# Both score products over all 128 rows: the keys' rounding remainder kept twice, and a smaller DMA scratch

## The chip, the cores and the metric

The kernel runs on one core of one Trainium2 chip. The metric is the device time of one execution in microseconds (us). Times of single instructions are in nanoseconds (ns) where the profile gives them so. TensorE is PE in the profile (PEld is its weight load), VectorE is DVE, ScalarE is ACT, GpSimd is POOL and SyncE is SP.

## The reference, cut to what matters

Three layers over 2048 tokens of width 1024: sliding-window attention, a gated recurrence, and a hybrid of two recurrences. The change touches the first layer alone. Its attention has 16 query heads of 64 in two groups of eight, two key/value heads, blocks of 128 queries, and a window that reaches into the block before:

```python
s = jnp.einsum('bqhgd,bkhd->bhgqk', qi, ki, preferred_element_type=jnp.float32) * scale
s = jnp.where(band & ((idx > 0) | (k_rel >= ATTN_BLOCK)), s, -jnp.inf)
m = jnp.maximum(jnp.max(s, axis=-1), sink)
p = jnp.exp(s - m[..., None])
p = p / (jnp.sum(p, axis=-1) + jnp.exp(sink - m))[..., None]
out = jnp.einsum('bhgqk,bkhd->bqhgd', p, vi)
```

## The kernel before

**Work and phases.** The 2048 tokens are cut into four quarters of 512. Each layer is worked a quarter at a time, in an order written out by hand (`00 01 10 02 d0 11 03 d1 ...`: layer, quarter), so attention stands in the first 480 us (quarters 0 and 1), around 825 to 1035 us (quarter 2) and around 1575 to 1800 us (quarter 3), beside other work.

**Products in two parts.** A float32 operand is kept as a rounded part (`F32R`, the name ends in `h` or the tile's first half) and as what the rounding left out (`l`). A projection is three products per 128 rows: hi·hi, hi·lo, lo·hi (`psA`, `psB`).

**Scores.** `attn_pair` works one query head of each group (`g` = 0, 1) at a time. Its tile `q[g]` (written in `q_evac`, named `qs` in the profile) has 128 rows: in the half `H2[g]` the rounded query of 64 rows, in the other half what its rounding left out. `kh[g]` holds the rounded key of key head `g` in both halves, so one product over 128 rows gives q_hi·k_hi + q_lo·k_hi. `kl` holds the key's remainder: key head 0 in rows 0 to 63, key head 1 in rows 64 to 127. A second product over the 64 rows `H2[g]` adds q_hi·k_lo to the same bank. A pair has 4 blocks (`block(b)`, 128 queries by up to 256 keys), a quarter has 8 pairs: 4·8·4·2 = 256 products with `kh` and 256 with `kl`.

**Behind the scores.** DVE adds the mask and takes the row maximum, ACT takes the exponential, DVE divides, PE transposes (`psPT`), ACT copies (`PT`), and PE multiplies with the values (`psO`).

**Keys.** `k_evac` runs once per quarter. From the second quarter on it first copies the last 128 columns of `kh` and `kl` to the front; then it rotates the key, and writes `kh` (four ACT copies of 64 rows x 512) and `kl` (two DVE subtractions).

**The order of the work.** The main thread (projections and output products) and side threads (`chains` for attention, `norms`, `ends`) are interleaved by a planner (`Pace`, `Threads`): each step has a due time from a table of costs, and a tile framework then places each engine's instructions. The planner's cost of an `F32R` product is its columns over 2400 MHz, whatever its rows.

All recorded operations have line L251 in the profile, so groups are read by tile names.

Of the kernel before, what the change touches and what calls it, by code (L numbers as in the profile page):

```python
# [10 lines left out]
F32 = mybir.dt.float32  # L11
F32R = mybir.dt.float32r
# [3 lines left out]
ALU = mybir.AluOpType  # L16
# [4 lines left out]
P = 128  # L21
D = 1024
TQ = 512
# [286 lines left out]
def rec_stack(ctx: ExitStack, tc: tile.TileContext, A, out, T=2048, layers=(0, 1, 2)):  # L310
    nc = tc.nc
    NPH = T // TQ
    pace = Pace(tc)
    te, ve, se, ge, sy = (pace.engine(e, n) for e, n in (
        (nc.tensor, "pe"), (nc.vector, "dve"), (nc.scalar, "act"), (nc.gpsimd, "pool"), (nc.sync, "dma")))
# [7 lines left out]
    st = ctx.enter_context(tc.tile_pool(name="st", bufs=1))  # L323
# [198 lines left out]
    H2 = [slice(0, 64), slice(64, 128)]  # L522
# [272 lines left out]
    if 0 in layers:  # L795
        aw, awo = A["attn_w_in"][0], A["attn_w_out"][0]
        ab = A["attn_b_in"][0]

        kh = [st.tile([P, P + TQ], F32R, name=f"kh{g}") for g in range(2)]
        kl = st.tile([P, P + TQ], F32R, name="kl")  # L800
        V0 = st.tile([P, 5, P], F32, name="V0")
    SWAP = [(i + 8 if i < 8 else i - 8) if i < 16 else i for i in range(32)]

# [53 lines left out]
    def layer0(i, ph, seq):  # L857

        S_ = {}

        def k_evac(ps):
            if ph:
                yield from need(("chain", seq - 1))
                for t in (*kh, kl):
                    se.copy(t[:, :P], t[:, TQ:].bitcast(F32))
                ve.tensor_copy(V0[:, 0], V0[:, 4])
            S_["tabs"] = yield from rope_tables(ph)
            k = yield from big.take([P, TQ], F32, "k0")
            yield from rope(k, ps, C["bkv"][:, 0:1], S_["tabs"])
            for g in range(2):  # L870
                for half in H2:
                    se.copy(kh[g][half, P:], k[H2[g]])
                ve.tensor_tensor(kl[H2[g], P:], k[H2[g]], kh[g][H2[g], P:].bitcast(F32), ALU.subtract)
            big.give(k)

        def v_evac(ps):
            vT = yield from big.take([P, TQ], F32, "vT")
            se.activation(out=vT, in_=ps, func=AF.Identity, bias=C["bkv"][:, 1:2])
            psd.give(ps)
            S_["vT"] = vT  # L880
            done.add(("v", i))

        def q_evac(pr):
            def go(ps):
                q = yield from big.take([P, TQ], F32, "q")
                yield from rope(q, ps, C["bq"][:, pr:pr + 1], S_["tabs"])

                S_["q", pr] = []
                for g in range(2):
                    t = yield from big.take([P, TQ], F32R, "qs")  # L890
                    se.copy(t[H2[g]], q[H2[g]])
                    ve.tensor_tensor(t[H2[1 - g]], q[H2[g]], t[H2[g]].bitcast(F32), ALU.subtract)
                    S_["q", pr].append(t)
                big.give(q)
                done.add(("q", i, pr))
                if pr == 7:
                    big.give(*S_["tabs"])
            return go

        def z_evac(pr):  # L900
            def go(ps):
                tz = yield from big.take([P, TQ], F32, "tz")
                se.activation(out=tz, in_=ps, func=AF.Tanh, bias=C["bzh"][:, pr:pr + 1], scale=0.5)
                ve.tensor_scalar(tz, tz, 0.5, 0.5, ALU.mult, ALU.add)
                ve.scalar_tensor_tensor(tz, ps, C["bz"][:, pr:pr + 1], tz, ALU.add, ALU.mult)
                psd.give(ps)
                S_["z", pr] = tz
                done.add(("z", i, pr))
            return go

        def w_out(half, cb):
            csl = slice(256 * cb, 256 * cb + 256)
            return 4, [(slice(64 * g, 64 * g + 64), slice(0, 256),
                        awo[512 * g + 256 * half:512 * g + 256 * half + 256, csl].rearrange("(k r) c -> r k c", r=64)) for g in range(2)], ("awo", half, cb)

        qs = [ch(i, w_ch(aw, 64 * pr, 512 + 64 * pr), q_evac(pr), ("chain", seq + pr - 2)) for pr in range(8)]
        zs = [ch(i, w_ch(aw, 1280 + 64 * pr, 1792 + 64 * pr), z_evac(pr), ("chain", seq + pr - 2)) for pr in range(8)]
        halves = [out_half(i, h, [w_out(h, cb) for cb in range(4)], A["attn_b_out"][0]) for h in range(2)]
        head = [ch_two(i, ch(i, w_ch(aw, 1024), k_evac), ch(i, w_ch(aw, 1152), v_evac)), qs[0], zs[0], qs[1]]
        body = []  # L920
        for pr in range(1, 6):
            body.append(zs[pr])
            if pr == 5:
                body += halves[0]
            body.append(qs[pr + 1])
        body += [zs[6], ch_two(i, qs[7], zs[7], True)]

        def chains():
            big.kept = 5
            yield from need(("v", i))  # L930
            yield pace.there(S_["vT"])
            ps = yield from bank(psm, "psV")
            for b in range(4):
                te.transpose(ps[:, P * b:P * b + P], S_["vT"][:, P * b:P * b + P], ident)
            yield
            se.copy(V0[:, 1:].rearrange("p a b -> p (a b)"), ps)
            psm.give(ps)
            big.give(S_["vT"])
            for pr in range(8):
                yield from attn_pair(ph, i, pr, S_)  # L940
                done.add(("chain", seq + pr))

        return head, body, halves[1], chains, 8

    def attn_pair(ph, i, pr, S_):
        yield from need(("q", i, pr))
        q = S_["q", pr]
# [3 lines left out]
        def block(b):  # L951

            k0 = 0 if (ph or b) else P
            S = yield from big.take([P, 2, 2 * P + 1], F32, "S", own=True)
            pss = []
            pss.append((yield from bank(psm, "psS", ahead=1)))
            pss.append((yield from bank(psm, "psS")))
            for g in range(2):
                te.matmul(pss[g][:, k0:2 * P], lhsT=q[g][:, P * b:P * b + P], rhs=kh[g][:, P * b + k0:P * b + 2 * P], start=True, stop=False)
            for g in range(2):  # L960
                te.matmul(pss[g][:, k0:2 * P], lhsT=q[g][H2[g], P * b:P * b + P], rhs=kl[H2[g], P * b + k0:P * b + 2 * P], start=False, stop=True)
            left[0] -= 1
            if not left[0]:
                big.give(*q)
            se.copy(S[:, :, 2 * P], C["sink"][:, pr])
            yield

            nm = sm.tile([P, 2], F32, tag="nm", name="nm")
            den = sm.tile([P, 2], F32, tag="den", name="den")
            for g in range(2):  # L970
                ve.tensor_tensor_reduce(out=S[:, g, k0:2 * P], in0=pss[g][:, k0:2 * P], in1=C["amask"][:, k0:], scale=-0.125,
                                        scalar=C["sink"][:, pr, g:g + 1], op0=ALU.add, op1=ALU.min, accum_out=nm[:, g:g + 1])
                psm.give(pss[g])
            yield
            for g in range(2):
                se.activation(out=S[:, g, k0:], in_=S[:, g, k0:], func=AF.Exp, bias=nm[:, g:g + 1], scale=-1.0, accum_out=den[:, g:g + 1])
            yield
            ve.reciprocal(den, den)
            for g in range(2):
                ve.tensor_scalar(S[:, g, k0:2 * P], S[:, g, k0:2 * P], den[:, g:g + 1], None, ALU.mult)  # L980
            yield
            bk = yield from bank(psm, "psPT")
            pt = bk.rearrange("p (k g q) -> p k g q", k=2, g=2)
            kbs = [1] if k0 else [0, 1]
            for kb in kbs:
                for g in range(2):
                    te.transpose(pt[:, kb, g], S[:, g, P * kb:P * kb + P], ident)
            big.give(S)
            yield
            PT = yield from big.take([P, 2, 2, P], F32, "PT", own=True)  # L990
            se.copy(PT[:, kbs[0]:], pt[:, kbs[0]:])
            psm.give(bk)
            yield
            if not po:
                po.append(None)
                po[0] = yield from bank(psm, "psO")
            if po[0] is None:
                yield lambda: po[0] is not None
            for kb in kbs:
                for g in range(2):  # L1000
                    te.matmul(po[0][64 * g:64 * g + 64, P * b:P * b + P], lhsT=V0[:, b + kb, 64 * g:64 * g + 64],
                              rhs=PT[:, kb, g], start=(kb == kbs[0]), stop=(kb == 1))
            big.give(PT)
# [859 lines left out]
```

## Time and profile before

| | |
|---|---|
| median of 3 runs | 3697.05 us (3694.93 to 3703.11) |
| the profiled execution's own time | 3696.45 us |
| its span, first to last instruction | 3694.7 us |
| mean granted clock of TensorE | 0.973 |
| PE, PEld, DVE, ACT, POOL busy | 95%, 80%, 65%, 35%, 12% |

The 1.75 us between the profiled execution's time and its span lie around the first and last instructions. A busy share is an average over stages that have different limits; and a matmul counts as busy from its start to its modelled end, so PE can be busy all the time and still have its matmuls far apart. The distance of matmul starts tells more than their durations.

### The profile page before, as it was taken

The numbers are of one execution on the slowest core, as the hardware profiler recorded it, in microseconds if no ns is written. First come the engines' busy times: TensorE is split into PE (matmuls) and PEld (weight loads), VectorE is DVE, ScalarE is ACT, GpSimd is POOL, SyncE is SP. The second block draws the span as 40 slices with busy tenths as digits, with TensorE's granted clock in tenths as the row PEclk, the third lists the DMA queues.
The fourth block names the chain that finished last, engine by engine and source line by source line (L and its number), as shares of the span: only waits on it lengthen the run. The fifth ranks groups of instructions, "written<-read, shape, count | busy, mean of one in ns | idle before, by whom it ended". The sixth has DMA issues, their size and how long they took to land. (4 is left out here: it accounts for less than half of the span.)

```text
span 3694.7 us, 75897 instructions
## 1 busy us (share of the span) xinstructions
PE 3521.4 (95%) x30488; PEld 2965.9 (80%) x30488; DVE 2402.3 (65%) x6735; ACT 1298.8 (35%) x3370; POOL 444.6 (12%) x649
## 2 busy tenths in 40 slices
PE   5999999989998999999999999999999999999998
PEld 4788887878887878877878787788778888878888
DVE  4666566466555677776666767665776765665675
ACT  4555433344432222343322223432232242334222
POOL 3421034421033000000000002110000010011000
PEclk8999999999998999999999999999999999999999
DMA  6766466755367444453575345485434457544665
GB/s 170 199 185 208 142 202 226 230 172 196 133 223 271 168 134 137 155 174 109 177 252 169 130 126 172 136 293 191 147 125 132 147 180 254 189 161 152 229 217 200
DMA packets 351104, 666.34 MB, mean 180 GB/s; under 512 B 164640, under 2 KB 246560, under 8 KB 298016
## 3 DMA queue, kind: packets, MB, share of 16 engines
q1 hardware_dynamic: 350752, 661.49, 54.1%
q8 instruction: 240, 3.93, 0.4%
q14 instruction: 112, 0.92, 0.1%
HBM read 494.42 MB, written 166.99 MB: 179 GB/s over the span
## 5 line engine op out<-in xcount | busy, mean ns | idle before, releaser
L251 PE MATMUL psA<-hth,wp 128*128 128x512 f32 (+1 forms) x5120 | 1560.6, 374 | 50.1 <-ACT wp L251 32.2
L251 PEld LDWEIGHTS psA<-hth,wp 128*128 128x128 f32 x5120 | 933.1, 193 | 218.7 <-ACT wp L251 33.7
L251 PE MATMUL psA<-htl,wp 128*128 128x512 f32 (+1 forms) x2560 | 935.3, 365 | 0.0
L251 PE MATMUL psB<-wp,mgh 128*128 128x256 f32 x3072 | 593.5, 292 | 14.3 <-DVE y L251 6.3
L251 PEld LDWEIGHTS psA<-htl,wp 128*128 128x128 f32 x2560 | 494.4, 193 | 62.2 <-issue 2.9
L251 PEld LDWEIGHTS psB<-wp,mgh 128*128 128x128 f32 x3072 | 487.6, 193 | 29.3 <-DVE y L251 7.8
L251 POOL TENSOR_TENSOR wp<-wf,wp 128x256 fp32r<-128x256 f32 x412 | 348.6, 877 | 934.8 <-ACT wp L251 827.1
L251 PE MATMUL psB<-wp,mgl 128*128 128x256 f32 x1536 | 443.5, 289 | 0.2 <-DVE mgl L251 0.2
L251 PE MATMUL psB<-wp,hth 128*128 128x256 f32 x1536 | 309.6, 297 | 4.3 <-DMA wp<-wk 3.9
L251 PEld LDWEIGHTS psB<-wp,mgl 128*128 128x128 f32 x1536 | 295.6, 193 | 3.3 <-issue 1.2
L251 PEld LDWEIGHTS psB<-wp,hth 128*128 128x128 f32 x1536 | 244.4, 194 | 13.5 <-issue 3.7
L251 PE MATMUL psB<-wp,htl 128*128 128x256 f32 x768 | 222.9, 290 | 0.0
L251 DVE TENSOR_TENSOR pr<-X,Mb 128x16 f32<-128x16 f32 (+30 forms) x496 | 205.2, 414 | 11.4 <-POOL Mb L251 1.7
L251 DVE TENSOR_TENSOR y<-psB,y 128x256 f32<-128x256 f32 x256 | 97.8, 419 | 111.8 <-PE psB L251 111.1
L251 DVE SCALAR_TENSOR_TENSOR Sbd<-Sbd,WC,psSt 64x64 f32<-64x64 f32 x256 | 71.4, 279 | 136.1 <-PE psSt L251 132.5
L251 ACT ACTIVATE S<-S,nm 128x257 f32<-128x257 f32 (+1 forms) x256 | 127.2, 499 | 82.9 <-DVE nm L251 82.0
L251 DVE TENSOR_REDUCE X<-pr 128x8 f32<-128x16 f32 (+30 forms) x496 | 146.6, 295 | 10.3
L251 ACT ACTIVATE junk<-y 128x1024 bf16<-128x1024 f32 (+1 forms) x128 | 94.5, 738 | 165.2 <-DVE y L251 154.4
L251 PEld LDWEIGHTS psB<-wp,htl 128*128 128x128 f32 x768 | 148.7, 194 | 2.5 <-issue 1.1
L251 DVE CUSTOM_DVE_ANT_0 S<-psS,amask,sink 128x256 f32<-128x256 f32 (+1 forms) x256 | 114.7, 471 | 41.2 <-PE psS L251 39.8
L251 DVE TENSOR_TENSOR QR<-QR,T 128x256 f32<-128x256 f32 x192 | 87.5, 456 | 80.0 <-PE psL L251 71.8
L251 POOL MEMSET Xt<- 32x256 f32 x32 | 9.7, 308 | 1055.8 <-PE psM L251 544.9
(283 smaller groups left out, 5442.6 us busy)
## 6 DMA issues: line engine op xcount, KB each, us to landing
wp<-wk SPq DMA_DIRECT2D x309, 1024.0 KB, 5.0
wk<-wp SPq DMA_DIRECT2D x103, 1024.0 KB, 5.0
xin<-x SPq DMA_DIRECT2D x48, 512.0 KB, 5.8
wf<-in_rec_w_in_dram SPq DMA_DIRECT2D x32, 512.0 KB, 6.3
x<-y SPq DMA_DIRECT2D x32, 512.0 KB, 6.1
wf<-in_w_in_dram SPq DMA_DIRECT2D x29, 512.0 KB, 6.7
ud<-um SPq DMA_DIRECT2D x52, 256.0 KB, 4.0
u<-ud SPq DMA_DIRECT2D x48, 256.0 KB, 3.2
```

The lines of the kernel that those rows point to most:

```text
L251: r = f(*a, **k)
```

## The change

`kl` becomes a list of two tiles, `kl[g]`. The remainder is still written by DVE into the half `H2[g]`, and an ACT copy puts it into the other half too. The second score product reads all 128 rows of `q[g]` and `kl[g]`, so it gives q_hi·k_lo + q_lo·k_lo. The two products of one `g` now follow each other in the code; before, both `kh` products came first. The carry at the start of a quarter copies four tiles instead of three. The program reserves 2048 bytes per partition for dynamic DMA instead of the default 16384; the second `kl` tile takes 2560.

```diff
--- before.py
+++ after.py
@@ -797,7 +797,7 @@
         ab = A["attn_b_in"][0]
 
         kh = [st.tile([P, P + TQ], F32R, name=f"kh{g}") for g in range(2)]
-        kl = st.tile([P, P + TQ], F32R, name="kl")
+        kl = [st.tile([P, P + TQ], F32R, name=f"kl{g}") for g in range(2)]
         V0 = st.tile([P, 5, P], F32, name="V0")
     SWAP = [(i + 8 if i < 8 else i - 8) if i < 16 else i for i in range(32)]
 
@@ -861,7 +861,7 @@
         def k_evac(ps):
             if ph:
                 yield from need(("chain", seq - 1))
-                for t in (*kh, kl):
+                for t in (*kh, *kl):
                     se.copy(t[:, :P], t[:, TQ:].bitcast(F32))
                 ve.tensor_copy(V0[:, 0], V0[:, 4])
             S_["tabs"] = yield from rope_tables(ph)
@@ -870,7 +870,8 @@
             for g in range(2):
                 for half in H2:
                     se.copy(kh[g][half, P:], k[H2[g]])
-                ve.tensor_tensor(kl[H2[g], P:], k[H2[g]], kh[g][H2[g], P:].bitcast(F32), ALU.subtract)
+                ve.tensor_tensor(kl[g][H2[g], P:], k[H2[g]], kh[g][H2[g], P:].bitcast(F32), ALU.subtract)
+                se.copy(kl[g][H2[1 - g], P:], kl[g][H2[g], P:].bitcast(F32))
             big.give(k)
 
         def v_evac(ps):
@@ -956,9 +957,8 @@
             pss.append((yield from bank(psm, "psS", ahead=1)))
             pss.append((yield from bank(psm, "psS")))
             for g in range(2):
-                te.matmul(pss[g][:, k0:2 * P], lhsT=q[g][:, P * b:P * b + P], rhs=kh[g][:, P * b + k0:P * b + 2 * P], start=True, stop=False)
-            for g in range(2):
-                te.matmul(pss[g][:, k0:2 * P], lhsT=q[g][H2[g], P * b:P * b + P], rhs=kl[H2[g], P * b + k0:P * b + 2 * P], start=False, stop=True)
+                for n, part in enumerate((kh, kl)):
+                    te.matmul(pss[g][:, k0:2 * P], lhsT=q[g][:, P * b:P * b + P], rhs=part[g][:, P * b + k0:P * b + 2 * P], start=(n == 0), stop=(n == 1))
             left[0] -= 1
             if not left[0]:
                 big.give(*q)
@@ -1843,7 +1843,7 @@
     import concourse.bacc as bacc
     from concourse.bass_utils import run_bass_kernel_spmd
 
-    nc = bacc.Bacc("TRN2", target_bir_lowering=False, num_devices=1)
+    nc = bacc.Bacc("TRN2", target_bir_lowering=False, num_devices=1, dynamic_dma_scratch_size=2048)
     arrays, args = {}, {}
 
     def add(key, name, a):
```

What stands in PE's order for two blocks of scores that follow an output projection (in the second quarter; `kh_89` and `kh_90` are the two key heads; the number behind a name is the tile's). Before:

```order
L251 MATMUL psB<-wp,mgl 128x256
L251 MATMUL psS<-kh_89,qs 128x256
L251 MATMUL psS<-kh_90,qs 128x256
L251 MATMUL psS<-kl,qs 128x256 x2
L251 MATMUL psS<-kh_89,qs 128x256
L251 MATMUL psS<-kh_90,qs 128x256
L251 MATMUL psS<-kl,qs 128x256 x2
L251 MATMUL psA<-hth,wp 128x512
L251 MATMUL psA<-htl,wp 128x512
```

and now (`kl_91` and `kl_92` are the two remainder tiles):

```order
L251 MATMUL psB<-wp,mgl 128x256
L251 MATMUL psS<-kh_89,qs 128x256
L251 MATMUL psS<-kl_91,qs 128x256
L251 MATMUL psS<-kh_90,qs 128x256
L251 MATMUL psS<-kl_92,qs 128x256
L251 MATMUL psS<-kh_89,qs 128x256
L251 MATMUL psS<-kl_91,qs 128x256
L251 MATMUL psS<-kh_90,qs 128x256
L251 MATMUL psS<-kl_92,qs 128x256
L251 MATMUL psA<-hth,wp 128x512
L251 MATMUL psA<-htl,wp 128x512
```

Before, the four products of a block stand as kh, kh, kl, kl; now as kh, kl, kh, kl. The count of products is the same.

At the end of the first quarter, PE's order where the scores stand between the products of a projection. Before:

```order
L251 MATMUL psA<-htl,wp 128x256
L251 MATMUL psS<-kh_90,qs 128x256
L251 MATMUL psPT<-ident,S 128x128
L251 MATMUL psS<-kl,qs 128x256
L251 MATMUL psPT<-ident,S 128x128
L251 MATMUL psA<-hth,wp 128x256
L251 MATMUL psS<-kh_89,qs 128x256
L251 MATMUL psS<-kl,qs 128x256
L251 MATMUL psA<-hth,wp 128x256
L251 MATMUL psS<-kh_90,qs 128x256
L251 MATMUL psS<-kl,qs 128x256
L251 MATMUL psA<-htl,wp 128x256
```

and now:

```order
L251 MATMUL psA<-hth,wp 128x256
L251 MATMUL psS<-kh_89,qs 128x256
L251 MATMUL psS<-kl_91,qs 128x256
L251 MATMUL psS<-kh_89,qs 128x256
L251 MATMUL psS<-kl_91,qs 128x256
L251 MATMUL psS<-kh_90,qs 128x256
L251 MATMUL psS<-kl_92,qs 128x256
L251 MATMUL psA<-hth,wp 128x256
L251 MATMUL psS<-kh_90,qs 128x256
L251 MATMUL psS<-kl_92,qs 128x256
L251 MATMUL psA<-htl,wp 128x256
```

Before, a pair kh, kl of one key head stands alone between products of the projection, and once a transpose lies between its two halves; now three pairs stand in a row and a fourth follows one product later.

What stands on ACT at the start of the third quarter (`k` is the rotated key, `qs` the query tile that the first score reads). Before:

```order
L251 CAST kh_89<-k_8773 64x512 x2
L251 ACTIVATE mt<-psO_8695,hrs 128x128 x4
L251 ACT_TABLE_LOAD
L251 ACTIVATE tz<-psA,bzh 128x512
L251 CAST kh_90<-k_8773 64x512 x2
L251 CAST mgh<-g_8381 128x512
L251 CAST qs<-q 64x512 x2
```

and now:

```order
L251 CAST kh_89<-k_8780 64x512 x2
L251 ACTIVATE mt<-psO_8701,hrs 128x128 x4
L251 ACT_TABLE_LOAD
L251 ACTIVATE tz<-psA,bzh 128x512
L251 CAST kl_91<-kl_91 64x512
L251 CAST kh_90<-k_8780 64x512
L251 CAST mgh<-g_8387 128x512
L251 CAST kh_90<-k_8780 64x512
L251 CAST qs<-q 64x512 x2
L251 CAST kl_92<-kl_92 64x512
```

The first copy of `kl` stands ahead of the copies of `kh_90`, and so ahead of the query's (`qs`); the second stands behind the query's.

## Rows read from the trace of the kernel before

**Rows 1.** The page's busy us (share of the span) xinstructions, PE to POOL.
```profile
PE 3521.4 (95%) x30488; PEld 2965.9 (80%) x30488; DVE 2402.3 (65%) x6735; ACT 1298.8 (35%) x3370; POOL 444.6 (12%) x649
```

**Rows 2.** Windows: busy us (instructions) of each engine, granted clock, DMA share, GB/s.
```profile
80.00:480.00 400.00, 390.38 (x2524) 315.61 (x2522) 267.60 (x729) 207.71 (x535) 89.00 (x104) 0.99 0.61 186
825.00:1035.00 210.00, 207.02 (x1302) 169.74 (x1303) 132.08 (x362) 96.17 (x255) 28.68 (x32) 0.94 0.49 168
1575.00:1800.00 225.00, 223.49 (x1548) 179.11 (x1550) 162.71 (x501) 99.02 (x276) 7.89 (x16) 0.98 0.42 141
480.00:825.00 345.00, 326.15 (x3544) 282.00 (x3543) 211.26 (x499) 119.69 (x272) 114.55 (x147) 0.98 0.64 208
1035.00:1575.00 540.00, 513.91 (x4990) 429.61 (x4989) 356.59 (x1028) 168.32 (x427) 59.87 (x92) 0.97 0.53 180
```

**Rows 3.** Tile psS: ns of one (min/median/max); who waited for its writers.
```profile
L251 PE MATMUL psS<-kh,qs x256: 221/282/580, 82.5 to 1796.5; 128*128 128x256 f32 x119, 128*128 128x128 f32 x9
...
L251 PE MATMUL psS<-kl,qs x256: 323/381/580, 82.7 to 1796.7; 64*128 64x256 f32 x119, 64*128 64x128 f32 x9
...
  DVE S L251: 39.8, 48
```

**Rows 4.** PE in order of time, 311.31 to 314.08: start us, us, instruction.
```profile
311.31 0.40 PE L251 MATMUL psB<-wp,mgh 128*128 128x256 f32 x2
311.55 0.28 PE L251 MATMUL psB<-wp,mgl 128*128 128x256 f32 x1
311.67 0.40 PE L251 MATMUL psS<-kh,qs 128*128 128x256 f32 x2
312.00 0.38 PE L251 MATMUL psS<-kl,qs 64*128 64x256 f32 x2
312.31 0.50 PE L251 MATMUL psS<-kh,qs 128*128 128x256 f32 x2
312.74 0.38 PE L251 MATMUL psS<-kl,qs 64*128 64x256 f32 x2
313.05 0.50 PE L251 MATMUL psA<-hth,wp 128*128 128x512 f32 x1
313.39 0.39 PE L251 MATMUL psA<-htl,wp 128*128 128x512 f32 x1
313.62 0.63 PE L251 MATMUL psA<-hth,wp 128*128 128x512 f32 x2
314.08 0.39 PE L251 MATMUL psA<-htl,wp 128*128 128x512 f32 x1
```

**Rows 5.** PE in order of time, 250.83 to 251.79, scores one by one.
```profile
250.83 0.39 PE L251 MATMUL psA<-hth,wp 128*128 128x256 f32 x1
251.05 0.28 PE L251 MATMUL psS<-kh,qs 128*128 128x256 f32 x1
251.26 0.38 PE L251 MATMUL psS<-kl,qs 64*128 64x256 f32 x1
251.57 0.39 PE L251 MATMUL psA<-htl,wp 128*128 128x256 f32 x1
251.79 0.40 PE L251 MATMUL psA<-hth,wp 128*128 128x256 f32 x2
```

**Rows 6.** Tiles kh and kl: the ScalarE copies, ns of one.
```profile
L251 ACT CAST kh<-k x16: 604/618/621, 77.0 to 1572.9; 64x512 fp32r<-64x512 f32 x16
...
L251 ACT CAST kl<-kl x3: 296/298/301, 83.0 to 1020.5; 128x128 fp32r<-128x128 f32 x3
```

**Rows 7.** PE in order of time: the first score of the third attention phase, and its wait.
```profile
825.08 0.38 PE L251 MATMUL psS<-kh,qs 128*128 128x256 f32 x1 [0.99 <-DVE qs L251]
```

**Rows 8.** Windows around one fall of the clock (columns as in Rows 2).
```profile
1010.00:1018.70 8.70, 6.30 (x52) 5.91 (x50) 8.64 (x10) 6.29 (x12) 7.59 (x8) 1.00 0.23 86
1018.70:1035.80 17.10, 17.10 (x62) 13.93 (x62) 9.79 (x31) 5.49 (x20) 1.03 (x1) 0.50 0.62 207
```

**Rows 9.** The page's DMA queues: packets, MB, share of 16 engines.
```profile
q1 hardware_dynamic: 350752, 661.49, 54.1%
```

## The prediction

> **What bounds the kernel now.** I first read the busy times: PE is busy for 3521.4 of 3694.7 us, DVE for 2402.3, ACT for 1298.8 [rows 1]. Next the windows of the stages, since the change touches attention alone. In its three stretches (400, 210 and 225 us) PE is busy for 390.4, 207.0 and 223.5 us: it stands idle for 14.1 of 835 us, 1.7%. In the two stretches between them it is idle for 18.9 of 345 and 26.1 of 540 us, 5.1% together [rows 2]. DVE, the next, is busy for 562.4 of the 835 us (67%). So attention is where PE sets the pace hardest, and its time there is worth most. The view of the score tile shows the other engines behind it: DVE waits 39.8 us, in 48 times, for scores [rows 3].
>
> A busy PE is not a PE at its peak, so I then went to the order of time and read distances between starts. Dense products of 256 columns start every 0.12 us (two and one from 311.31 to 311.67), those of 512 columns every 0.23 (from 313.39 to 314.08, three) [rows 4]. Around the `kl` products this breaks. The view of the tile gives the odd sign: the product over 64 rows takes 381 ns in the median, the one over 128 rows 282 [rows 3].
>
> **What a kl product costs today.** Take a pair alone between projection products [rows 5]. The projection product at 250.83 is followed by kh after 0.22 us instead of 0.12, kh by kl after 0.21 instead of 0.12, and kl by the next projection product after 0.31 instead of 0.12. The next one again takes 0.22 (251.57 to 251.79), so this is a period: 0.74 us for three products that would need 0.36. Excess: 0.38 us, of which 0.09 lies ahead of kl, 0.19 behind it, and 0.10 behind the first full product after it.
>
> Where two kl products follow each other (block 312.31 to 313.05 [rows 4]) the second takes no time: the row holds both in 0.38 us, as long as one. The four products take 0.74 us where four dense ones take 0.48. Excess: 0.26 us. The exit costs here too: the projection product at 313.05 takes 0.34 to the next instead of 0.23, which the period counts at its head.
>
> This is not the cost of adding into one bank: the projections do that at 0.12 and 0.23. It goes with the change from 128 to 64 rows and back.
>
> In the program's order of before, 146 kl products stand alone and 55 times two are side by side (146 + 110 = 256). So the excess is 146 x 0.38 + 55 x 0.26 = 55.5 + 14.3 = **69.8 us**.
>
> **What the change removes.** All 256 second products now have 128 rows, the form of the kh product and of its dense neighbours. By the dense rows [rows 4] each should take 0.12, and its neighbours no extra. Bounds: at best the whole 69.8 us go; at worst nothing, if the gaps come from something else than the row count. I take all of it, since products of the same shape run at 0.12 on either side of the scores. The weights are loaded as often as before, 30488 loads for 30488 products [rows 1].
>
> **What it adds.** Eight ACT copies of 64x512; the nearest row is the same copy of kh, 618 ns [rows 6]: 4.9 us. Three carry copies of 296 ns [rows 6]: 0.9 us. ACT is busy 402.9 of the 835 us [rows 2], so most is hidden under its idle time. Not at a quarter's start: there by the new order the query's copy `qs` is queued behind the first kl copy in the first and third quarters and behind both in the second, and in the fourth the next query's evacuation is behind both; the first score waits for `qs`, 0.99 us in the third quarter [rows 7]. Price: 0 if other matmuls cover it, at most 0.62 + 1.24 + 0.62 + 1.24 = 3.7 us; I take 3, since PE already waits there. DVE's work is unchanged. No product is added.
>
> **The scratch.** No row shows what it does. Traffic is 661.49 MB on one queue, which SP issues [rows 9]; GpSimd issues none in this program. A gain I exclude, since less room can't shorten a transfer; I take 0 and leave a few us of loss in the range.
>
> **What comes back.** Once PE is 70 us quicker, softmax and evacuations have less time behind each product. Today 14.1 us of the 835 are PE's idle time. If the shortened 765 us went to the 5.1% of the neighbouring stretches [rows 2], idle time would be 39 us: 25 given back. DVE's share would go from 67 to 562.4/765 = 74%, no bound. Between 0 and 25 I take 10, nearer to none, because all three stretches lie below 2.5% now.
>
> **The sum.** -69.8 + 3 + 10 = -57 us: 3696.45 - 57 = 3639.5 for the profiled execution, which lies 0.6 us under the median of the runs; so **3640 us**, 1.5% less.
>
> **Rivals.**
>
> *More than the excess: the clock.* At 1018.7 us the clock falls to half (granted 0.50, so 1.2 GHz) and stays for 17.1 us; ahead of that PE had been busy 6.30 of 8.70 us, and through the low stretch scores stand between the projection's products [rows 8]. If the switches keep it low, the change gives back half of such stretches: the three attention windows have 0.99, 0.94 and 0.98 [rows 2], so 0.01 x 400 + 0.06 x 210 + 0.02 x 225 = 21 us of lost clock, at most. Half of it, and nothing given back elsewhere: 3697 - 70 - 10 + 3 = 3620. Against: a wait of PE starts the fall, and shorter work leaves more waits.
>
> *Less: the chains take over.* If softmax on DVE and ACT limited a block soon after, 25 us would come back, and the copies would be exposed in full: 3697 - 70 + 25 + 4 = 3656; with new falls of the clock up to 3675. For it: DVE is at 72% in the last attention stretch [rows 2].
>
> *No change: PE was not the limit.* Then 3690 to 3704. Against: 1.7% idle. It would show as PE's idle time growing by what its products lose.
>
> *Slower: two half-height products run at once.* The row of the two kl products shows it: 0.38 us for both, the second free [rows 4]. The change gives that up in 55 places, 55 x 0.12 = 6.6 us, and adds 3 of copies: 3707. It decides if less than about a seventh of the 69.8 us is due to the row count: below 10 us the loss is larger. The Trainium skill, "TensorEngine Tiling (Array Packing)", section "Key Properties", states this as a rule: different tiles load weights and multiply in parallel; by it all 128 pairs could overlap, and the change would cost 128 x 0.12 = 15 us. The same section says that changing the tiling mode drains the engine. The trace agrees with both, and prices them: 0.12 us won by a second product, 0.26 net lost by its block [rows 4].
>
> **How the numbers follow.** Forecast (3625 to 3655): 0.58. Clock, below 3625: 0.13. Chains take over, 3655 to 3690: 0.19. No change: 0.05. Slower: 0.05. No change here means within 0.2% (7.4 us), about what a measurement of this kernel can tell. The likeliest case's own range is 3625 to 3655; 3610 to 3680 leaves out the unchanged and the slower case and the ends of two others, and holds 0.83. Faster: 0.58 + 0.13 + 0.19 = 0.90; same 0.05; slower 0.05.
>
> **What the next profile should show.** The kl products at 128 rows with a median like kh's 282 ns; kh to kl at 0.12 us in the order of time, and the first projection product behind at 0.12 or 0.23; no 0.31 after kl. The attention stretches shorter by about 55 us in total, the work between and behind them at its old length within 10 us. PE's idle time in attention between 14 and 40 us. ACT busy longer by 6 us. I would be wrong if kl stayed at 0.21 after kh (then the gap is not the row count), if PE's waits for `qs` or `PT` rose to tens of us, or if the gain in attention were lost behind 1800 us, where another order of the same work could cost or save.

## The result, and the profile after

The changed kernel takes 3636.07 us (median of 4 runs, 3631.12 to 3637.53), the one before 3700.08 us beside it: the ratio is 0.9826, with a 95% interval of 0.9809 to 0.9843. Forecast were 3640 us and a range of 3610 to 3680. Timed again beside the experiments, the ratio was 0.9821 (0.9797 to 0.9845).

The page's busy line after the change, which answers to [rows 1]:

```profile
PE 3455.2 (95%) x30488; PEld 2942.9 (81%) x30488; DVE 2399.4 (66%) x6735; ACT 1303.3 (36%) x3381; POOL 446.7 (12%) x649
```

PE, as busy in share as before, has lost 66.2 us of busy time with the same 30488 matmuls and weight loads; DVE has the same work, and ACT 4.5 us more with its eleven new copies.

The view of the score tile after the change (ns of one, min/median/max; at the end who waited for its writers, in us and times), which answers to [rows 3]:

```profile
L251 PE MATMUL psS<-kh,qs x256: 222/282/583, 82.2 to 1731.5; 128*128 128x256 f32 x120, 128*128 128x128 f32 x8
...
L251 PE MATMUL psS<-kl,qs x256: 273/280/420, 82.4 to 1731.6; 128*128 128x256 f32 x120, 128*128 128x128 f32 x8
...
  DVE S L251: 8.6, 10
```

The kl product has 128 rows now and takes 280 ns in the median in place of 381, like kh. DVE's waits for scores have gone from 39.8 us to 8.6.

PE in order of time after the change (start us, us, instruction), at the place of [rows 4]:

```profile
302.06 0.28 PE L251 MATMUL psS<-kh,qs 128*128 128x256 f32 x1
302.18 0.28 PE L251 MATMUL psS<-kl,qs 128*128 128x256 f32 x1
302.30 0.28 PE L251 MATMUL psS<-kh,qs 128*128 128x256 f32 x1
...
302.88 0.28 PE L251 MATMUL psS<-kl,qs 128*128 128x256 f32 x1
303.00 0.40 PE L251 MATMUL psA<-hth,wp 128*128 128x512 f32 x1
303.23 0.39 PE L251 MATMUL psA<-htl,wp 128*128 128x512 f32 x1
```

Every start is 0.12 us after the one ahead of it, and in the projection behind the distance is 0.23; nothing of the 0.21, 0.31 and 0.34 of before is left. From the first score to the projection it is 0.94 us for eight products, before 1.38 (311.67 to 313.05).

For the balance I cut the three attention stretches from their first score to their last, and add the time behind the last. Windows of the kernel before (busy us and instructions of PE, PEld, DVE, ACT, POOL; granted clock; DMA share; GB/s):

```profile
82.50:476.70 394.20, 384.57 (x2489) 310.92 (x2488) 263.16 (x714) 203.09 (x523) 88.29 (x103) 0.99 0.61 186
825.10:1031.80 206.70, 203.81 (x1289) 166.74 (x1289) 129.73 (x355) 94.93 (x251) 28.68 (x32) 0.94 0.49 171
1575.00:1796.80 221.80, 220.29 (x1522) 176.21 (x1522) 160.66 (x493) 96.77 (x268) 7.89 (x16) 0.98 0.42 143
1796.80:3694.70 1897.90, 1820.86 (x16402) 1556.01 (x16402) 1241.21 (x3565) 581.67 (x1573) 116.99 (x211) 0.98 0.54 180
```

and of the changed kernel:

```profile
82.20:452.70 370.50, 359.30 (x2485) 305.85 (x2486) 260.79 (x711) 203.97 (x528) 89.67 (x103) 0.98 0.64 196
800.10:982.70 182.60, 178.31 (x1289) 156.01 (x1290) 128.16 (x349) 93.74 (x250) 29.39 (x32) 0.99 0.54 185
1525.20:1731.70 206.50, 201.69 (x1523) 169.49 (x1523) 158.97 (x488) 97.78 (x269) 7.90 (x16) 1.00 0.45 154
1731.70:3633.90 1902.20, 1824.38 (x16403) 1557.30 (x16402) 1242.91 (x3569) 582.71 (x1575) 115.93 (x211) 0.98 0.53 180
```

The stretches are 23.7, 24.1 and 15.3 us shorter, 63.1 together. PE's busy time in them falls from 808.7 to 739.3 us, 69.4 less; its idle time grows from 14.0 to 20.3. Behind the last score the same work takes 4.3 us more (1902.2 for 1897.9), and the stretches between change by 1 us or less, so that 60.8 us are left of the span. The granted clock needs a look too. Within the stretches it is 1.00 but for whole pieces at 0.50; these sum to 36.9 us before and 17.0 after, and PE is busy in nearly all of them (36.6 and 16.6 us). At 0.50 TensorE has 1.2 in place of 2.4 GHz, so half of such time is lost, at most: 18.5 us before and 8.5 after. So about 10 of the 69.4 us come from a clock that was low for less time, and about 59 from the products themselves. (The windows round the clock to 0.01, which is 4 us of a stretch of 400. Below, too, the time lost to the clock is therefore half of the pieces at 0.50.)

### The profile page after: what moved, and what is told of

Its sections match the earlier page's. It is cut to its first block, busy times and chain, and to the rows that moved or that the text cites. A ratio compares the mean times of both kernels' runs of the same rounds, so it can differ in the third digit from the quotient of the medians.

```text
span 3633.9 us, 75918 instructions
## 1 busy us (share of the span) xinstructions
PE 3455.2 (95%) x30488; PEld 2942.9 (81%) x30488; DVE 2399.4 (66%) x6735; ACT 1303.3 (36%) x3381; POOL 446.7 (12%) x649
## 5 line engine op out<-in xcount | busy, mean ns | idle before, releaser
L251 ACT CAST wp<-wf 128x1024 fp32r<-128x1024 f32 x103 | 107.9, 1049 | 78.5 <-PE psB L251 58.6
```

Source lines behind the costliest of these rows:

```text
L251: r = f(*a, **k)
```

## The experiments

Each kernel was timed beside the kernel before; of the ratios the interval is at 95%.

**Order alone.** The two products of one head follow each other as in the change, but kl stays one tile and 64 rows:

```diff
             for g in range(2):
                 te.matmul(pss[g][:, k0:2 * P], lhsT=q[g][:, P * b:P * b + P], rhs=kh[g][:, P * b + k0:P * b + 2 * P], start=True, stop=False)
-            for g in range(2):
                 te.matmul(pss[g][:, k0:2 * P], lhsT=q[g][H2[g], P * b:P * b + P], rhs=kl[H2[g], P * b + k0:P * b + 2 * P], start=False, stop=True)
```

> The kernel before with one thing changed: the two score products of one head follow each other (kh, kl, kh, kl), kl still over 64 rows in one tile. In this program all 256 kl products stand alone, before 146 did and 55 times two were side by side. Theory (the cost is the change between 128 and 64 rows and back): 256 x 0.38 = 97.3 us of excess in place of 69.8, so 27 us slower than before, about 3727 us. Rival 1 (a 64-row product is slow by itself, wherever it stands): no change, about 3700. Rival 2 (the gain came from the new order): about 3636.

Measured: 3732.0 us, ratio 1.009 (1.0067 to 1.0113), 33 us slower than before, where 27 were expected. Both rivals fall: the time does change, and the order alone brings no gain but loses. Its windows over the attention stretches (columns as above):

```profile
82.20:496.50 414.30, 406.70 (x2488) 322.21 (x2487) 263.44 (x714) 204.27 (x523) 87.80 (x103) 0.97 0.57 178
845.00:1057.20 212.20, 209.86 (x1288) 169.34 (x1288) 129.67 (x355) 95.38 (x251) 28.65 (x32) 0.95 0.48 167
1600.80:1827.60 226.80, 225.51 (x1522) 178.74 (x1521) 160.25 (x490) 96.97 (x268) 6.99 (x16) 0.98 0.41 140
```

Together they are 853.3 us, 93.7 more than in the changed kernel, with nearly the same instruction counts. The granted clock loses 26.9 us of them, 18.4 more than after the change. The rest, 75.3 us over 256 lone kl products, is 0.29 us for each.

This run alone leaves a third reading: a 64-row product could be slow by itself unless a second one runs beside it. The kernel before holds the answer in another layer, where sixteen products over 64 rows, of 128 columns each, follow one another; only three of them start together with the one ahead. PE in order of time:

```profile
2353.63 0.28 PE L251 MATMUL psB<-wp,mgl 128*128 128x256 f32 x1
2353.84 1.71 PE L251 MATMUL psA<-q,k 64*128 64x128 f32 x16
2355.47 0.51 PE L251 MATMUL psB<-wp,mgh 128*128 128x256 f32 x2
2355.82 0.28 PE L251 MATMUL psB<-wp,mgl 128*128 128x256 f32 x1
```

The sixteen take 1.63 us up to the next full-row product, 0.10 each, where a lone kl product, of twice the columns, takes 0.31. The price stands at the two ends: 0.21 us ahead of the first, and 0.35 for the two full-row products behind the last, which need 0.24 elsewhere (311.31 to 311.55 [rows 4]). So the cost comes with the change of rows.

**Half of it.** Head 1's kl product over 64 rows again:

```diff
                 for n, part in enumerate((kh, kl)):
-                    te.matmul(pss[g][:, k0:2 * P], lhsT=q[g][:, P * b:P * b + P], rhs=part[g][:, P * b + k0:P * b + 2 * P], start=(n == 0), stop=(n == 1))
+                    rows = H2[g] if n == 1 and g == 1 else slice(0, P)
+                    te.matmul(pss[g][:, k0:2 * P], lhsT=q[g][rows, P * b:P * b + P], rhs=part[g][rows, P * b + k0:P * b + 2 * P], start=(n == 0), stop=(n == 1))
```

> The changed kernel, but head 1's kl product again over 64 rows (head 0's over 128): 128 kl products are left as a lone change of rows. Leaves out q_lo x k_lo for head 1, as the kernel before did. Theory (each lone kl costs 0.38 us): 128 x 0.38 = 48.6 us come back, so about 3680, 19 us under before: half of the edit gives less than a third of the gain, since the products that stood side by side are now apart. Rival (the cost goes by the number of 64-row products): half of the gain, about 3668.

Measured: 3679.73 us, ratio 0.9947 (0.9929 to 0.9966), 20 us under before, 19 expected; the rival's half of the gain (a ratio of 0.991) lies outside the interval. One block shows both forms side by side, PE in order of time:

```profile
311.34 0.38 PE L251 MATMUL psS<-kh,qs 128*128 128x256 f32 x1
311.56 0.28 PE L251 MATMUL psS<-kl,qs 128*128 128x256 f32 x1
311.68 0.28 PE L251 MATMUL psS<-kh,qs 128*128 128x256 f32 x1
311.89 0.38 PE L251 MATMUL psS<-kl,qs 64*128 64x256 f32 x1
312.20 0.50 PE L251 MATMUL psA<-hth,wp 128*128 128x512 f32 x1
312.53 0.39 PE L251 MATMUL psA<-htl,wp 128*128 128x512 f32 x1
```

The kl product of head 0 stands 0.22 us behind its kh, since the kh at 311.34 itself follows a kl over 64 rows, and the next kh 0.12 behind that kl. The kl product of head 1, over 64 rows, comes 0.21 us after its kh, and the next product 0.31 after it, which in turn takes 0.33 where the projection's own distance is 0.23. The three parts of the price (0.09, 0.19, 0.10) stand where the prediction had them, on either side of one product. The windows of its attention stretches:

```profile
82.70:471.40 388.70, 378.47 (x2485) 311.49 (x2484) 261.32 (x714) 204.57 (x529) 89.38 (x103) 0.99 0.61 188
818.80:1013.50 194.70, 190.68 (x1289) 160.61 (x1289) 129.68 (x354) 95.01 (x253) 28.84 (x32) 0.98 0.51 181
1557.10:1773.20 216.10, 213.01 (x1523) 173.90 (x1522) 160.31 (x491) 97.77 (x269) 7.39 (x16) 0.99 0.44 147
```

799.5 us, 39.9 more than after the change; with 1.7 of them from the clock (10.2 us lost in place of 8.5), it is 0.30 us for each of 128 kl products.

**One quarter.** The kl products over 64 rows in the third quarter alone, in the same order on every engine:

```diff
                 for n, part in enumerate((kh, kl)):
-                    te.matmul(pss[g][:, k0:2 * P], lhsT=q[g][:, P * b:P * b + P], rhs=part[g][:, P * b + k0:P * b + 2 * P], start=(n == 0), stop=(n == 1))
+                    rows = H2[g] if n == 1 and ph == 2 else slice(0, P)
+                    te.matmul(pss[g][:, k0:2 * P], lhsT=q[g][rows, P * b:P * b + P], rhs=part[g][rows, P * b + k0:P * b + 2 * P], start=(n == 0), stop=(n == 1))
```

> The changed kernel with the kl products over 64 rows in the third quarter alone (64 of 256), in the same order on every engine as in the changed kernel. Leaves out q_lo x k_lo there. Theory: 64 x 0.38 = 24.3 us come back, about 3660. If the changes of rows also hold the clock low, the low-clock time in that stretch goes from 3.4 us to 10 or more, and the time to 3664 to 3670; if low clock comes only from waits of TensorE, it stays at about 3.4 us and the time at 3655 to 3660.

Measured: 3658.19 us, ratio 0.988 (0.9863 to 0.9898), by the ratios 20 us over the changed kernel. The windows:

```profile
82.80:452.10 369.30, 358.77 (x2486) 305.51 (x2486) 260.17 (x710) 202.74 (x525) 89.65 (x103) 0.98 0.64 196
799.40:1004.10 204.70, 202.53 (x1289) 164.36 (x1289) 128.59 (x352) 95.88 (x253) 28.25 (x32) 0.98 0.48 167
1544.70:1750.70 206.00, 201.64 (x1523) 169.48 (x1523) 158.80 (x488) 97.57 (x269) 7.87 (x16) 1.00 0.45 154
```

The first and the third window are within 1.2 us of the changed kernel's; the second is 22.1 us longer, for 64 products. 1.7 of that is clock: the piece at 0.50 in it lasts 6.8 us, where the changed kernel has 3.4. The rest is 0.32 us for each. On the clock the run doesn't decide, since it shows neither 10 us of low clock nor the old value. Why it is less than 0.38 can be seen at the head of the stretch. This kernel, PE in order of time, five pairs from 799.43 to 802.56:

```profile
799.43 0.38 PE L251 MATMUL psS<-kh,qs 128*128 128x256 f32 x1
799.74 0.38 PE L251 MATMUL psS<-kl,qs 64*128 64x256 f32 x1
800.05 0.39 PE L251 MATMUL psS<-kh,qs 128*128 128x256 f32 x1
...
802.56 0.50 PE L251 MATMUL psB<-wp,mgh 128*128 128x256 f32 x2
```

and the changed kernel, the same five pairs from 800.10 to 801.69:

```profile
800.10 0.39 PE L251 MATMUL psS<-kh,qs 128*128 128x256 f32 x1
800.32 0.28 PE L251 MATMUL psS<-kl,qs 128*128 128x256 f32 x1
800.44 0.28 PE L251 MATMUL psS<-kh,qs 128*128 128x256 f32 x1
800.55 0.28 PE L251 MATMUL psS<-kl,qs 128*128 128x256 f32 x1
800.82 0.39 PE L251 MATMUL psS<-kh,qs 128*128 128x256 f32 x1
801.04 0.28 PE L251 MATMUL psS<-kl,qs 128*128 128x256 f32 x1
...
801.69 0.40 PE L251 MATMUL psB<-wp,mgh 128*128 128x256 f32 x2
```

With 64 rows every step is 0.31 us: 3.13 us for the five pairs. With 128 rows they take 1.59, not the 1.2 of ten dense products: 0.27 us pass from 800.55 to 800.82, and the first product behind that pause takes 0.22. So 0.31 us are saved for each pair here, and 0.07 go to short pauses that the slow products had covered. They are too short to show as PE's idle time, since a matmul counts as busy for 0.28 us, but the weight load of the product at 800.82 shows what the pause was, a wait for the query tile that DVE writes:

```profile
800.82 0.19 PEld L251 LDWEIGHTS psS<-kh,qs 128*128 128x128 f32 x1 [0.19 <-DVE qs L251]
```

**No second product.** To ask whether PE still sets the pace after the change:

```diff
-                for n, part in enumerate((kh, kl)):
-                    te.matmul(pss[g][:, k0:2 * P], lhsT=q[g][:, P * b:P * b + P], rhs=part[g][:, P * b + k0:P * b + 2 * P], start=(n == 0), stop=(n == 1))
+                te.matmul(pss[g][:, k0:2 * P], lhsT=q[g][:, P * b:P * b + P], rhs=kh[g][:, P * b + k0:P * b + 2 * P], start=True, stop=True)
```

> The changed kernel without the second score product: leaves out q x k_lo altogether (256 products of 0.12 us; kl is still written). If TensorE still sets the pace of attention after the change, nearly all of 256 x 0.12 = 30.7 us goes: 3606 to 3615. If the softmax chains have taken over, as the rival on what comes back had it, less than half goes: over 3620.

Measured: 3603.83 us, ratio 0.974 (0.9722 to 0.9759), by the ratios 32 us under the changed kernel, for 30.7 us of products; that is a little below the range expected. The windows:

```profile
83.00:434.30 351.30, 341.24 (x2366) 289.05 (x2365) 258.85 (x710) 202.33 (x525) 87.55 (x103) 0.99 0.66 206
783.10:956.80 173.70, 170.70 (x1221) 147.66 (x1220) 124.92 (x344) 92.10 (x246) 26.64 (x32) 0.99 0.56 196
1499.10:1697.50 198.40, 193.69 (x1473) 165.51 (x1473) 158.45 (x489) 97.28 (x267) 7.42 (x16) 0.98 0.47 160
```

723.4 us in place of 759.6, with 11.0 us lost to the clock in place of 8.5. PE's idle time is 17.8 us, no more than after the change. The softmax chains have not taken over; PE still sets the pace.

**The scratch alone.** The kernel before with the smaller reservation; the order on every engine is that of before:

```diff
-    nc = bacc.Bacc("TRN2", target_bir_lowering=False, num_devices=1)
+    nc = bacc.Bacc("TRN2", target_bir_lowering=False, num_devices=1, dynamic_dma_scratch_size=2048)
```

> The kernel before with the smaller DMA scratch alone; the order on every engine is that of before. Theory: no difference from before, within 0.2%, DMA landing times and queue shares as before. Rival (the scratch is part of what moved the time): outside 0.2%.

Measured: 3702.14 us, ratio 0.9999 (0.9982 to 1.0016): nothing. Its DMA queue, against [rows 9]:

```profile
q1 hardware_dynamic: 350752, 661.49, 53.9%
```

The packets and bytes are the same, the share 53.9% for 54.1%.

**The copies.** Two kernels take the eight ACT copies away from the changed kernel; the changed kernel itself ran beside them.

> The changed kernel, unchanged, as the reference for the two beside it: about 3636 us, ratio to before 0.982 to 0.984.

It took 3638.47 us, ratio 0.9821 (0.9797 to 0.9845). In the first of the two, the second half holds zeros from the first quarter on:

```diff
-                se.copy(kl[g][H2[1 - g], P:], kl[g][H2[g], P:].bitcast(F32))
+                if ph == 0:
+                    ve.tensor_tensor(kl[g][H2[1 - g], P:], k[H2[g]], k[H2[g]], ALU.subtract)
```

> The changed kernel, but the second half of each kl tile holds zeros, written once by VectorE in the first quarter, in place of the eight ScalarE copies: the second product is over 128 rows and leaves out q_lo x k_lo, as before. Theory: the copies cost 0 to 4 us on the path at the quarters' starts, so 3632 to 3636. Rival (the copies delay the query tiles and are what was given back): 3625 or less.

Measured: 3633.98 us, ratio 0.9811 (0.9786 to 0.9836). In the second, VectorE writes both halves:

```diff
-                ve.tensor_tensor(kl[g][H2[g], P:], k[H2[g]], kh[g][H2[g], P:].bitcast(F32), ALU.subtract)
-                se.copy(kl[g][H2[1 - g], P:], kl[g][H2[g], P:].bitcast(F32))
+                for half in H2:
+                    ve.tensor_tensor(kl[g][half, P:], k[H2[g]], kh[g][H2[g], P:].bitcast(F32), ALU.subtract)
```

> The changed kernel, but VectorE writes the second half of each kl tile too, by the same subtraction (eight more of about 0.69 us), in place of the ScalarE copies; the values are the same. Theory: ScalarE's queue is freed of 4.9 us and VectorE gets 5.5 us, both mostly under other work, so 3632 to 3640. Rival (VectorE is the nearer bound at a quarter's start): 3640 to 3645.

Measured: 3637.05 us, ratio 0.9822 (0.9797 to 0.9846). All three lie in each other's intervals. The rival of 3625 or less is not borne out, nor that VectorE is the nearer bound; whether the copies cost nothing or the 4.5 us that two medians differ by is below what these runs tell apart, and no version is shown to beat the changed kernel.

## Why the prediction was right, point by point

- **PE bounds attention.** Right, and still so after the change: 30.7 us of products taken away bring 32.
- **A lone kl costs 0.38 us, two side by side 0.26.** Right where it stands, and it is the change of rows, not the row count by itself: the order alone, which parts the 55 pairs, loses 33 us; half the edit gains 20 of 64; and sixteen 64-row products in a row run at 0.10 us each. The Trainium skill, "TensorEngine Tiling (Array Packing)", section "Key Properties", says that a change of the tiling mode drains TensorE. The block with both forms fits that: 0.09 us ahead of the product, 0.19 behind it, 0.10 on the product after that; no run shows how much of this is the draining. The other rule that the Trainium skill gives there, that different tiles work in parallel, was the slower rival. The trace agrees that it happens; the pairs saved 0.12 us each by it and paid more for being entered and left, and with all 256 apart the kernel was slower still.
- **69.8 us go.** The dense distance came out as taken, but the term was too large in effect: lone products are worth 0.29 to 0.32 us each in three kernels, some 80% of 0.38. The rest is the next point.
- **10 us come back.** The term was too small: 6.3 us come back as idle time, and some 11 more are missing (69.8 less the 59 that the balance leaves). The five pairs above show where such time goes, into pauses too short to be shown as idle that had been in the old time too, under the slow products; that all 11 us went there is not shown. Beside this the work behind the last score took 4.3 us more, within the 10 that the prediction allowed and outside its sum.
- **The clock.** The rival of at most 21 us was given 0.13 as a case of its own; about 10 us of it came in the profiled execution beside the forecast, whose sum holds nothing for it. Without them the profiled execution (3635.79 us) would have stood near 3646, inside the range and 6 us over its forecast of 3639.5. So the clock made up for the point above, and part of the closeness of 3636 to 3640 is luck of two terms that cancel.
- **3 us for copies.** Not told apart from nothing, and no run contradicts the bound of 3.7.
- **Scratch: 0.** Right.
- **No change, or the chains take over.** Neither: the stretches shrank by 63.1 us (about 55 were foretold), and idle time rose to 20.3, in the foretold 14 to 40.

What stays open is whether the low clock belongs to the changes of rows. The mean granted clock of every execution is on record; what it falls short of 1 by, times the span, is the time lost in the whole program. The averages are 114 us with all 256 kl products alone (4 executions), 104 in the kernel before (24) and the same with the small scratch (12), 98 with 128 lone products (4), 91 with 64 (4), and 84 to 90 in the changed kernel and the two without copies (6 to 10 each). Executions of one kernel scatter by some 8 us around these. So the clock's part of the gain, 14 us by these averages, isn't a chance of one execution, and it goes with the number of changes. But without second products, with no change of rows in the scores at all, 96 us are lost (4). No run kept the products and changed TensorE's waits alone.

## What to carry to other kernels

In this kernel a product over half the rows between full-row products cost more than a full one. Where you meet such a product, look at the starts of its neighbours, not at its own duration, and if the other half can be filled with something harmless (zeros did as well here) or useful, fill it. Count how often the form changes in the program's order: two halves side by side, or sixteen in a row, pay only once. And don't count on the whole of a saving on the pacing engine: of the lone products' price some 80% came back, since slow instructions can cover pauses that no idle time shows, while the second products, taken away whole, brought all of their 30.7 us.

## What the runs showed of the hardware that was not expected

The low clock is not fixed by the order of the work. The kernel before, and the same order with the small scratch, lose their clock in different stretches. The windows of the latter:

```profile
82.20:486.00 403.80, 393.86 (x2488) 317.80 (x2487) 264.72 (x718) 203.21 (x523) 88.16 (x103) 0.96 0.59 183
835.90:1033.90 198.00, 195.69 (x1289) 160.16 (x1287) 127.91 (x352) 94.24 (x250) 28.99 (x32) 0.99 0.49 173
1574.60:1796.10 221.50, 220.10 (x1523) 175.92 (x1522) 159.83 (x491) 96.26 (x268) 7.90 (x16) 0.98 0.42 143
```

Granted are 0.96, 0.99 and 0.98, where the kernel before had 0.99, 0.94 and 0.98, and the lengths follow: 403.8 and 198.0 us in place of 394.2 and 206.7. Two stretches of one order of work moved by 9 us in opposite directions with hardly any change of the whole, so a single stretch of one execution can't be read to better than that when the clock differs.

The weight loads show a part of the price. Two of the kernel before, at the place of [rows 5], and one of the changed kernel, at the place of the scores shown first:

```profile
251.26 0.18 PEld L251 LDWEIGHTS psS<-kl,qs 64*128 64x128 f32 x1
251.57 0.19 PEld L251 LDWEIGHTS psA<-htl,wp 128*128 128x128 f32 x1
302.06 0.19 PEld L251 LDWEIGHTS psS<-kl,qs 128*128 128x128 f32 x1
```

The loads of the first two start with their products, at 251.26 and 251.57: neither ran ahead of the change of rows, into 64 or out of them. The load at 302.06 starts 0.12 us ahead of its product at 302.18, while the product before it runs. Behind the pause at 800.82 load and product start together too, and the next product comes after 0.22 us, without any change of rows, as it does behind the product at 251.57. How much of the 0.38 us is the load no run separates.
